# Experts' stage of a hybrid attention and mixture-of-experts block: the order of three engines written out, and a ring of 128x1024 split buffers

## The chip, the cores and the metric

The kernel runs on one core of a Trainium2 chip. The metric is the device time of one execution in microseconds, from launch to end. Three runs of the kernel before took 1589.34, 1589.37 and 1590.09 us, so the median is 1589.37 us.

## The reference

One layer over 1024 tokens of width 1024, all in float32: a token mixer (differential attention beside a causal pooling branch, merged by gates), a layer norm, a mixture of experts, a second layer norm. Only the mixture matters here:

```
g_p, g_idx = top_k(softmax(x @ w_router_group + b), 1)         # one of 4 groups
e_p, e     = top_k(softmax(expert logits of that group), 2)    # two of its 8 experts
weights    = g_p * e_p / sum(e_p)
for each expert e, for its rows xs:
    gate, up = split(xs @ w_gate_up[e], 2)                     # 1024 -> 2 x 512
    y = (silu(gate) * up) @ w_down[e]                          # 512 -> 1024
out[token] += weight * y
x = layer_norm(ALPHA * x + out)
```

## The kernel before

**Split products.** TensorE multiplies in the format fp32r, which keeps fewer bits than float32. So every operand A is split into A = hi + lo: ScalarE casts A to fp32r (hi, L150) and VectorE subtracts (lo = A - hi, L151). The helper `split` at L149 does both, and `mm3` (L164 to L167) issues three matmuls, hi*hi, hi*lo and lo*hi, into one PSUM tile.

**The experts' stage** takes the stretch from about 940 us to 1536 us. Each of the 32 experts has room for 96 rows (CAP). Its weights come from HBM in six pieces of 1 MB, 128 x 2048 float32: pieces 0 and 1 hold the gate half of `w_gate_up`, 2 and 3 the up half, 4 and 5 the two column halves of `w_down`. A piece holds four chunks of 128 x 512, one per block of 128 contraction rows. `stream` (L1044) lists the 192 pieces in the order of use, in which an expert's two down pieces stand behind the gate and up pieces of the next expert. `ahead(n)` (L1049) issues their loads on SyncE's queue in that order, each into one of NS + NM = 15 + 3 slots; a load waits until the piece 18 places earlier has been split.

For an expert, GpSimd gathers 96 rows of the normalised tokens (`gather`, L1081, tile `xg`, four buffers). TensorE turns them by eight 96x128 transposes into PSUM (tile `X`, L1039), and `split` makes `xT`. Then come `gu_half` for the gate (24 matmuls) and for the up half (24 matmuls), each into a PSUM tile `gu`; `hidden` (L1094: Silu on ScalarE, a multiplication on VectorE, tile `h`); four transposes of `h` and their split into `hT`; and `down` (24 matmuls into two PSUM tiles `dn`, each weighted into `y` by ScalarE at L1104, then a scattering DMA with addition into Y, L1105). So an expert has 72 matmuls and 12 transposes on TensorE.

**The weights' split** is done chunk by chunk: `weights_(e, c, g)` (L1061) makes one 128x512 chunk into one of five buffers `wh`, just ahead of the matmuls that use it (`product`, L1070); the first five chunks are made before the first expert (PRE = 5).

**The order of the work** in this stage is not written out. The framework's planner puts each engine's instructions in an order of its own, by program order as priority and by estimated times. In the profiled execution that order is, on TensorE: 48 gate and up matmuls, 4 down matmuls, the four transposes of this expert's `h`, the eight transposes of an `xg`, the other 20 down matmuls. `count` (L1112) works out, with three small matmuls and some VectorE operations, how many experts have more than 96 rows; `overflow` (L1136) is a loop over those. No instruction of the loop's body shows up in the trace: it runs zero times.

Of the kernel before, what the change touches and what calls it, by code (L numbers as in the profile page):

```python
# [11 lines left out]
F32 = mybir.dt.float32  # L12
# [32 lines left out]
NM = 3  # L45
M_AT = (13, 16, 17)
PRE = 5
MOE_ENG = ()
# [5 lines left out]
COUNT_AT = 1  # L54
# [55 lines left out]
def body(tc, ctx, A, out):  # L110
# [922 lines left out]
    def transposed(src, n, name, t=None):  # L1033

        t = t or turn_to(n, name)
        for g in range(0, n, 4):
            p = pt([4, CAP], "X", 3)
            for k in range(4):
                PE.transpose(p[:, k], src[:, (g + k) * 128:(g + k) * 128 + 128], ident[:CAP, :CAP])  # L1039
            split(t[:, 0, g:g + 4], t[:, 1, g:g + 4], p)  # L1040
        return t
# [17 lines left out]
    split_ = {}  # L1059

    def weights_(e, c, g):  # L1061

        if (e, c, g) in split_:
            return split_[e, c, g]
        ahead(stream.index((e, c)) + 1)
        h = split_[e, c, g] = mt([2, 512], "wh", F32R, WH_BUFS)
        split(h[:, 0], h[:, 1], pieces[e, c][:, g])
        return h

    def product(ps, x, e, c, k0):  # L1070

        for g in range(4):
            h, k = weights_(e, c, g), k0 + g
            mm3(ps, (x[:, 0, k], x[:, 1, k]), (h[:, 0], h[:, 1]), k == 0, k == (3 if c >= 4 else 7))
# [13 lines left out]
    def gu_half(e, x, c):  # L1088
        ps = pt([512], "gu", 3, CAP)
        product(ps, x, e, c, 0)  # L1090
        product(ps, x, e, c + 1, 4)
        return ps

    def hidden(h, g, u):  # L1094
        ACT.activation(h, g, AF.Silu)
        DVE.tensor_mul(h, h, u)
        return h

    def down(e, hT):
        y = rt([D], "y", F32, Y_BUFS)  # L1100
        for n in range(2):
            d = pt([512], "dn", 2, CAP)
            product(d, hT, e, 4 + n, 0)
            ACT.activation(y[:, n * 512:n * 512 + 512], d, AF.Copy, scale=wgt[:, expert[e]:expert[e] + 1])  # L1104
# [5 lines left out]
        ysc.append(q)  # L1110

    def count():  # L1112

        pc = pt([2 + 2 * NE + 1], "X", 3)
        v, b = mt([3], "cv", F32, 1)[:NE], mt([2 * NE + 1], "cb", BF, 1)[:NE]
        nb, end = v[:, 0:1], v[:, 1:2]

        PE.matmul(pc[:NE, 0:1], cum, one[:, 0:1], start=True, stop=True)
        DVE.tensor_scalar(nb, pc[:NE, 0:1], 1.0 / CAP, -0.5 - 0.5 / CAP, op0=OP.mult, op1=OP.add)
        DVE.tensor_scalar(nb, nb, MAGIC, MAGIC, op0=OP.add, op1=OP.subtract)  # L1120
        DVE.tensor_scalar(nb, nb, 0.0, None, op0=OP.max)
        DVE.tensor_copy(b[:, 2 * NE:], nb)
        PE.matmul(pc[:NE, 1:2], tri[:NE, :NE], b[:, 2 * NE:], start=True, stop=True)
        DVE.tensor_add(end, pc[:NE, 1:2], nb)
# [3 lines left out]
        po = pc[:1, 2:]  # L1128
        PE.matmul(po, one[:NE, 0:1], b, start=True, stop=True)
        ov, ovi = mt([NE], "ov", F32, 1)[:1], mt([2 * NE + 1], "ovi", I32, 1)[:1]  # L1130
# [3 lines left out]
        return ovi  # L1134

    def overflow(x, ovi):  # L1136

        n_more = nc.values_load(ovi[0:1, 2 * NE:], min_val=0, max_val=MAXB)
        with tc.For_i(0, n_more, 1) as i:
# [10 lines left out]
            def flat(src, n, name):  # L1150
                t = extra([n, CAP], name)
# [7 lines left out]
            def whole(ps, x, c, k0, last):  # L1159
                w = extra([4, 512], "we")  # L1160
# [9 lines left out]
            h = extra([512], "h")[:CAP]  # L1170
# [18 lines left out]
    with ExitStack() as order_:  # L1189
        if MOE_ENG:  # L1190
            order_.enter_context(tc.manual_schedule(engines=set(getattr(mybir.EngineType, n) for n in MOE_ENG)))
        x, h = turn_to(8, "xT"), rt([512], "h", F32, 1)
        ahead(NS + NM)
        for g in range(PRE):
            weights_(0, g // 4, g % 4)
        transposed(gx.pop(0), 8, "xT", x)
        for e in range(NE):
            if e == COUNT_AT:
                ov = count()
            if e + NXG < NE:  # L1200
                gx[e + NXG] = gather(e + NXG)
            g = gu_half(e, x, 0)
            hT = transposed(h, 4, "hT") if e else None
            u = gu_half(e, x, 2)
            hidden(h, g, u)
            if e + 1 < NE:
                x = transposed(gx.pop(e + 1), 8, "xT")
# [173 lines left out]
```

## Time and profile before

The profiled execution took 1583.73 us. Its span, from the first to the last instruction, is 1581.9 us, which leaves 1.8 us around it. It lies 5.6 us below the median of the three runs.

| what | whole span | experts' stage, 1100 to 1400 us |
|---|---|---|
| TensorE busy | 95% | 100% |
| VectorE busy | 77% | 92% |
| ScalarE busy | 63% | 89% |
| GpSimd busy | 21% | 44% |
| granted TensorE clock | 0.978 | 1.00 |
| moved by DMA | 241 GB/s | 376 to 384 GB/s, 16 engines busy all the time |

A busy share is the time in which at least one instruction of the engine was running. Matmuls overlap, so TensorE at 100% means that there is no gap between them, not that each runs at its peak: what a matmul costs is the distance between the starts of two that follow each other.

### The profile page before, as it was taken

The page shows a single profiled execution, that of the slowest core. Times are in us where ns is not written, and L with a number is a line of the kernel's source. Part 1 is how long each engine was busy: PE and PEld are TensorE (multiplying, and loading weights), DVE is VectorE, ACT ScalarE, POOL GpSimd, SP SyncE. Part 2 cuts the span into 40 slices and gives each one's busy share as a digit, 9 for nine tenths or more (in the row PEclk, how much of TensorE's full clock was granted, in tenths as well). Part 3 has the DMA queues.
Part 4 walks back from the last instruction along what each step waited for, and adds up shares of the span by engine and source line. Part 5 has one row for each costly group of instructions (what it writes and reads, how often), then busy time and mean ns, then how long its engine had stood idle before and what let it go on. Part 6 is the DMA issues. An engine that isn't in the chain of part 4 may idle for free.

```text
span 1581.9 us, 23148 instructions
## 1 busy us (share of the span) xinstructions
PE 1504.2 (95%) x7627; PEld 1188.8 (75%) x7627; DVE 1219.3 (77%) x2670; ACT 989.0 (63%) x1955; POOL 336.4 (21%) x232
## 2 busy tenths in 40 slices
PE   8999999999999999999999969999999999999970
PEld 6988888898898898888887856666666666666640
DVE  5774125988988986675567779899999899999867
ACT  4423124676676676674331128888888888888874
POOL 0001000210211210100004440344444444440010
PEclk9999999999999999999999969999999999999995
DMA  7156224855755864427475588999999999999725
GB/s 234 62 175 197 73 80 134 231 191 164 220 190 139 242 193 138 121 97 281 186 283 196 178 290 302 371 381 384 382 385 373 375 380 382 384 380 374 252 31 213
DMA packets 117034, 381.29 MB, mean 241 GB/s; under 512 B 12759, under 2 KB 43863, under 8 KB 91520
## 3 DMA queue, kind: packets, MB, share of 16 engines
q1 hardware_dynamic: 76176, 304.83, 51.5%
q0 software_dynamic: 40160, 74.14, 18.2%
q8 instruction: 61, 1.00, 0.3%
q10 hardware_dynamic: 576, 0.83, 0.2%
q14 instruction: 61, 0.50, 0.1%
HBM read 314.01 MB, written 71.35 MB: 244 GB/s over the span
## 4 chain that ended last, share of the span: by engine, by line
PE 84%; issue 7%; DVE 5%; DMA 2%; ACT 1%; POOL 1%; DVEq 0%; POOLq 0%; SPq 0%; ACTq 0%
PE gu L167 6%; PE gu L166 6%; PE gu L165 6%; PE ps L577 4%; PE pg L165 4%; PE pg L166 4%; PE pg L167 4%; PE po L628 3%; PE dn L166 3%; PE dn L167 3%; PE dn L165 3%; PE X L1039 2%; PE pv L165 2%; PE tp L613 2%; PE pv L167 2%
## 5 line engine op out<-in xcount | busy, mean ns | idle before, releaser
L151 DVE TENSOR_TENSOR wh<-we,wh 128x512 fp32r<-128x512 f32 x768 | 473.0, 683 | 13.6 <-ACT wh L150 10.4
L150 ACT CAST wh<-we 128x512 fp32r<-128x512 f32 x768 | 433.9, 621 | 24.8 <-PE gu L167 6.5
L1083 POOL DMA_INDIRECT xg<-X,idx x32 | 159.9, 4998 | 277.1 <-PE X L1039 266.9
L167 PE MATMUL gu<-wh,xT 128*96 128x512 f32 x512 | 202.8, 396 | 0.0
L165 PE MATMUL gu<-wh,xT 128*96 128x512 f32 x512 | 202.2, 395 | 0.5 <-ACT xT L150 0.5
L166 PE MATMUL gu<-wh,xT 128*96 128x512 f32 x512 | 202.1, 395 | 0.0
L151 DVE TENSOR_TENSOR w<-wraw,w 128x512 fp32r<-128x512 f32 x111 | 75.8, 687 | 92.6 <-ACT w L150 92.2
L150 ACT CAST w<-wraw 128x512 fp32r<-128x512 f32 x111 | 68.5, 621 | 117.7 <-PE pg L167 38.5
L580 ACT ACTIVATE P<-ps,stat 128x256 f32<-128x256 f32 (+7 forms) x128 | 94.8, 741 | 54.7 <-DVE stat L579 53.8
L166 PEld LDWEIGHTS gu<-wh,xT 128*96 128x96 f32 x512 | 83.1, 162 | 36.4
L165 PEld LDWEIGHTS gu<-wh,xT 128*96 128x96 f32 x512 | 83.0, 162 | 36.1 <-ACT xT L150 0.5
L167 PEld LDWEIGHTS gu<-wh,xT 128*96 128x96 f32 x512 | 83.0, 162 | 36.0 <-DVE xT L151 0.5
L166 PE MATMUL dn<-wh,hT 128*96 128x512 f32 x256 | 103.3, 404 | 1.6 <-DVE wh L151 1.5
L165 PE MATMUL dn<-wh,hT 128*96 128x512 f32 x256 | 100.8, 394 | 1.7 <-ACT wh L150 1.7
L167 PE MATMUL dn<-wh,hT 128*96 128x512 f32 x256 | 100.8, 394 | 0.0
L165 PE MATMUL pg<-xT,w 128*128 128x512 f32 x256 | 100.5, 392 | 0.0
L166 PE MATMUL pg<-xT,w 128*128 128x512 f32 x256 | 99.9, 390 | 0.0
L167 PE MATMUL pg<-xT,w 128*128 128x512 f32 x256 | 99.8, 390 | 0.0
L577 PE MATMUL ps<-K,Q 128*128 128x512 f32 (+2 forms) x384 | 98.8, 364 | 0.8 <-DVE z L464 0.8
L579 DVE TENSOR_REDUCE stat<-ps 128x1 f32<-128x256 f32 (+7 forms) x128 | 95.6, 748 | 1.1
L165 PE MATMUL pv<-w,xT 128*128 128x256 f32 x256 | 72.8, 284 | 0.0
L577 PEld LDWEIGHTS ps<-K,Q 128*128 128x128 f32 x384 | 64.7, 189 | 10.7 <-DVE z L464 1.3
(279 smaller groups left out, 3397.3 us busy)
## 6 DMA issues: line engine op xcount, KB each, us to landing
we<-in_we_dram SPq DMA_DIRECT2D x192, 1024.0 KB, 13.6
wraw<-in_w_dram SPq DMA_DIRECT2D x61, 512.0 KB, 3.8
Q<-RQ POOLq DMA_DIRECT2D x64, 256.0 KB, 5.1
RQ<-rh SPq DMA_DIRECT2D x32, 256.0 KB, 3.4
K<-RK POOLq DMA_DIRECT2D x16, 512.0 KB, 4.2
V<-RV POOLq DMA_DIRECT2D x16, 512.0 KB, 5.7
OT<-ohl SPq DMA_DIRECT2D x48, 128.0 KB, 2.3
oT<-OT POOLq DMA_DIRECT2D x6, 1024.0 KB, 10.5
```

The costliest lines, as they stand in the source:

```text
L150: ACT.copy(hi, src)
L151: DVE.tensor_sub(lo, src, r(hi))
L165: PE.matmul(ps, a[0], b[0], start=start, stop=False)
L166: PE.matmul(ps, a[0], b[1], start=False, stop=False)
L167: PE.matmul(ps, a[1], b[0], start=False, stop=stop)
L577: PE.matmul(ps[:, c:c + n], q[:, o, m, qc], Kt[h, m][:, c:c + n], start=o == 0, stop=o == 1)
L579: DVE.tensor_reduce(st_[:, m:m + 1], ps[:, :W], AX.X, OP.max, negate=True)
L580: ACT.activation(Pt[h, i][m][:, :W], ps[:, :W], AF.Exp, bias=st_[:, m:m + 1], accum_out=st_[:, 2 + m:3 + m])
L613: PE.transpose(ps[:, k], p[:, (4 * g + k) * 128:(4 * g + k) * 128 + 128], ident)
L628: PE.matmul(o[:, 0, c], Vt[h][:, a, kt], aT[kt // 4][:, kt % 4, b, c], start=j == 0, stop=j == len(parts) - 1)
L1039: PE.transpose(p[:, k], src[:, (g + k) * 128:(g + k) * 128 + 128], ident[:CAP, :CAP])
L1083: q = POOL.indirect_dma_start(out=x, out_offset=None, in_=X1, in_offset=IO(ap=idx[:, 2 * (e < NXG), expert[e]:expert[e] + 1], axis=0), bou ...
```

## The change

The experts' loop is put under a manual schedule for TensorE, ScalarE and VectorE: in it these three engines run exactly in program order. The program is rearranged to go with it. The weights are split by halves of a piece (two chunks, 128x1024) into a ring of five buffers; a count `used` goes up by one after each half's six matmuls, the next half is split there, and other operations are put into a table `todo` to be written one to three halves later. Two of the 18 load slots go (NM 3 to 1). The transposes of `h` stand behind the next expert's gate half, those of `xg` behind the up half. `count` becomes a generator whose steps are written over ten halves of expert 1, with its PSUM tile taken from tag `gu`. The overflow loop's tiles come from the slots.

```
-NM = 3
-M_AT = (13, 16, 17)
-PRE = 5
-MOE_ENG = ()
+NM = 1
+M_AT = (13,)
 WH_BUFS = 5
...
-    def transposed(src, n, name, t=None):
+    def transposes(src, n):
+        ps = []
         for g in range(0, n, 4):
-            p = pt([4, CAP], "X", 3)
+            ps.append(pt([4, CAP], "X", 3))
             for k in range(4):
-                PE.transpose(p[:, k], src[...], ident[:CAP, :CAP])
-            split(t[:, 0, g:g + 4], t[:, 1, g:g + 4], p)
-        return t
+                PE.transpose(ps[-1][:, k], src[...], ident[:CAP, :CAP])
+        return ps
+
+    def taken(t, g, p):
+        split(t[:, 0, 4 * g:4 * g + 4], t[:, 1, 4 * g:4 * g + 4], p)
...
+    parts = [(e, c, g) for e, c in stream for g in range(2)]
+    ring = deque()
+    todo = {}
+
+    def split_next():
+        if state["split"] < len(parts):
+            e, c, g = parts[state["split"]]
+            state["split"] += 1
+            ahead(stream.index((e, c)) + 1)
+            h = mt([2, 2, 512], "wh", F32R, WH_BUFS)
+            split(h[:, 0], h[:, 1], pieces[e, c][:, 2 * g:2 * g + 2])
+            ring.append(h)
+
+    def put(n, f, *a):
+        todo.setdefault(state["used"] + n, []).append(partial(f, *a))
+
+    def product(ps, x, c, k0):
+        for g in range(2):
+            h = ring.popleft()
+            for i in range(2):
+                k = k0 + 2 * g + i
+                mm3(ps, (x[:, 0, k], x[:, 1, k]), (h[:, 0, i], h[:, 1, i]), k == 0, k == (3 if c >= 4 else 7))
+            state["used"] += 1
+            split_next()
+            for f in todo.pop(state["used"], ()):
+                f()
...
+    with tc.manual_schedule(engines={mybir.EngineType.PE, mybir.EngineType.Activation, mybir.EngineType.DVE}):
         x, h = turn_to(8, "xT"), rt([512], "h", F32, 1)
         ahead(NS + NM)
+        for _ in range(WH_BUFS):
+            split_next()
+        for g, p in enumerate(transposes(gx.pop(0), 8)):
+            taken(x, g, p)
         for e in range(NE):
+            if e == 1:
+                counting, found = count(), []
+                for n in (1, 2, 5, 6, 9, 10):
+                    put(n, lambda: found.append(next(counting)))
             if e + NXG < NE:
                 gx[e + NXG] = gather(e + NXG)
+            g = gu_half(x, 0)
+            if e:
+                hT = turn_to(4, "hT")
+                put(1, taken, hT, 0, transposes(h, 4)[0])
+            put(2, ACT.activation, h, g, AF.Silu)
+            u = gu_half(x, 2)
             if e + 1 < NE:
+                x = turn_to(8, "xT")
+                for i, p in enumerate(transposes(gx.pop(e + 1), 8)):
+                    if e:
+                        put(1 + i, taken, x, i, p)
+                    else:
+                        taken(x, i, p)
+            put(3 if 0 < e < NE - 1 else 1, DVE.tensor_mul, h, h, u)
             if e:
                 down(e - 1, hT)
+        hT = turn_to(4, "hT")
+        taken(hT, 0, transposes(h, 4)[0])
+        down(NE - 1, hT)
+        for n in sorted(todo):
+            for f in todo.pop(n):
+                f()
+    ov = found[-1]
     ln2 = slot([2, D], F32, "ln2")
...
-    down(NE - 1, transposed(h, 4, "hT"))
     overflow(xgs[0], ov)
```

`down` now puts each weighting (`weighted`, with the scatter behind the second) one half later by `put(1, ...)`.

## Rows read from the trace of the kernel before

**Rows 1.** Stretches, all engines: start:end, length, busy time (count) by engine, clock, DMA.

```profile
1010.00:1500.00 490.00, 490.00 (x2248) 338.19 (x2249) 450.40 (x752) 437.36 (x806) 188.92 (x50) 1.00 1.00 372
```

**Rows 2.** Timeline, all engines: start, duration, engine, line, operation, count, [idle before <- releaser].

```profile
1210.55 0.39 PE L165 MATMUL dn<-wh,hT 128*96 128x512 f32 x1
...
1210.80 0.36 PEld L1039 LDWEIGHTS X<-cst,h 96*128 96x128 f32 x4 [0.32 <-DVE h L1096]
1210.81 0.55 PE L1039 MATMUL X<-cst,h 96*128 96x96 f32 x4
...
1211.32 1.03 PE L1039 MATMUL X<-cst,xg 96*128 96x96 f32 x8
1211.60 6.70 DVE L151 TENSOR_TENSOR wh<-we,wh 128x512 fp32r<-128x512 f32 x11
...
1212.62 6.53 POOL L1083 DMA_INDIRECT xg<-X,idx  x1 [10.05 <-PE X L1039]
1212.64 0.40 PE L167 MATMUL dn<-wh,hT 128*96 128x512 f32 x1
...
1228.86 0.39 PE L165 MATMUL dn<-wh,hT 128*96 128x512 f32 x1
```

**Rows 3.** Chain of waits, experts' stage: start, duration, engine, tile, line, count.

```profile
1009.54 1.41 PE X L1039 x12
...
1412.32 1.41 PE X L1039 x12
```

**Rows 4.** Timeline of TensorE, early in the stage.

```profile
987.32 0.39 PE L165 MATMUL gu<-wh,xT 128*96 128x512 f32 x1
987.55 0.49 PE L1039 MATMUL X<-cst,xg 96*128 96x96 f32 x4
987.83 0.45 PE L166 MATMUL gu<-wh,xT 128*96 128x512 f32 x1
988.12 0.39 PE L167 MATMUL gu<-wh,xT 128*96 128x512 f32 x1
```

**Rows 5.** Timeline of TensorE, second block from the end.

```profile
1505.27 0.47 PE L166 MATMUL dn<-wh,hT 128*96 128x512 f32 x1 [0.98 <-DVE wh L151]
```

**Rows 6.** Groups by line and form, 0 to 120 us: line, engine, operation, count | busy, mean ns.

```profile
L151 DVE TENSOR_TENSOR xT<-xr,xT 128x1024 fp32r<-128x1024 f32 x8 | 9.8, 1225 | 6.2 <-ACT xT L150 6.2
L150 ACT CAST xT<-xr 128x1024 fp32r<-128x1024 f32 x8 | 8.4, 1051 | 12.0 <-DMA xr<-in_xT_dram 12.0
```

**Rows 7.** Groups by line and form, 1010 to 1500 us.

```profile
L151 DVE TENSOR_TENSOR wh<-we,wh 128x512 fp32r<-128x512 f32 x646 | 396.7, 683 | 4.3 <-ACT wh L150 2.8
L150 ACT CAST wh<-we 128x512 fp32r<-128x512 f32 x646 | 364.1, 621 | 9.9
```

**Rows 8.** Timeline of ScalarE, start of the stage.

```profile
936.78 1.66 ACT L150 CAST wh<-we 128x512 fp32r<-128x512 f32 x3 [3.86 <-DMA Y<-yy]
941.75 0.48 ACT L150 CAST xT<-X 128x384 fp32r<-128x384 f32 x1 [3.31 <-PE X L1039]
```

**Rows 9.** Timeline of TensorE, start of the stage.

```profile
945.19 0.90 PE L1039 MATMUL X<-cst,xg 96*128 96x96 f32 x4 [2.84 <-DMA xg<-X,idx]
945.80 0.72 PE L165 MATMUL gu<-wh,xT 128*96 128x512 f32 x1
...
959.67 0.47 PE L165 MATMUL gu<-wh,xT 128*96 128x512 f32 x1 [0.46 <-ACT xT L150]
```

**Rows 10.** Timeline, all engines, end of the stage.

```profile
1529.19 0.47 PE L165 MATMUL dn<-wh,hT 128*96 128x512 f32 x1 [1.66 <-ACT wh L150]
...
1529.92 0.47 PE L166 MATMUL dn<-wh,hT 128*96 128x512 f32 x1 [0.25 <-DVE wh L151]
...
1535.71 0.39 PE L167 MATMUL dn<-wh,hT 128*96 128x512 f32 x1
```

**Rows 11.** Loads of the weights, from 1000 us on: count, issue ns, first and last issue.

```profile
L1055 SPq DMA_DIRECT2D we<-in_we_dram x157: 327/328/328, 1001.8 to 1480.1; - x157
```

**Rows 12.** Time from issue to landing of those loads, us.

```profile
DMA to landing us min/median/max: 8.8/14.2/19.2
```

More of the change, by code (lines that the diff above doesn't have):

```diff
@@ L53 @@
 NXG = 4
-COUNT_AT = 1
 ROPE_POOL = (1,)
@@ L1057, in ahead @@
             pieces[e, c] = w
[L1059 to L1074, printed above, removed]
+    parts = [(e, c, g) for e, c in stream for g in range(2)]
[21 more added lines that the diff above has]
+                f()
     ahead(13)
@@ L1086, in gather, with gu_half, scatter @@
         return x
-    def gu_half(e, x, c):
+    def gu_half(x, c):
         ps = pt([512], "gu", 3, CAP)
-        product(ps, x, e, c, 0)
-        product(ps, x, e, c + 1, 4)
-        return ps
[L1094 to L1104, printed above, removed]
+        product(ps, x, c, 0)
+        product(ps, x, c + 1, 4)
+        return ps
+    def scatter(e, y):
         q = POOL.indirect_dma_start(out=Y, out_offset=IO(ap=idx[:, 1, expert[e]:expert[e] + 1], axis=0), in_=y, in_offset=None,
@@ L1110, in down, with weighted @@
         ysc.append(q)
+    def weighted(e, y, n, d):
+        ACT.activation(y[:, n * 512:n * 512 + 512], d, AF.Copy, scale=wgt[:, expert[e]:expert[e] + 1])
+        if n:
+            scatter(e, y)
+    def down(e, hT):
+        y = rt([D], "y", F32, Y_BUFS)
+        for n in range(2):
+            d = pt([512], "dn", 2, CAP)
+            product(d, hT, 4 + n, 0)
+            put(1, weighted, e, y, n, d)
     def count():
-        pc = pt([2 + 2 * NE + 1], "X", 3)
+        pc = pt([512], "gu", 3)[:, :2 + 2 * NE + 1]
+        ov, ovi = mt([NE], "ov", F32, 1)[:1], mt([2 * NE + 1], "ovi", I32, 1)[:1]
         v, b = mt([3], "cv", F32, 1)[:NE], mt([2 * NE + 1], "cb", BF, 1)[:NE]
@@ L1122, in count @@
         DVE.tensor_copy(b[:, 2 * NE:], nb)
+        yield
         PE.matmul(pc[:NE, 1:2], tri[:NE, :NE], b[:, 2 * NE:], start=True, stop=True)
+        yield
         DVE.tensor_add(end, pc[:NE, 1:2], nb)
@@ L1128, in count @@
         po = pc[:1, 2:]
+        yield
         PE.matmul(po, one[:NE, 0:1], b, start=True, stop=True)
-        ov, ovi = mt([NE], "ov", F32, 1)[:1], mt([2 * NE + 1], "ovi", I32, 1)[:1]
+        yield
         DVE.tensor_copy(ovi, po)
@@ L1133, in count @@
         DVE.tensor_scalar(ovi[:, NE:2 * NE], ov, 1.0, float(CAP), op0=OP.add, op1=OP.mult)
-        return ovi
+        yield ovi
     def overflow(x, ovi):
@@ L1150, in flat @@
             def flat(src, n, name):
-                t = extra([n, CAP], name)
+                t = slot([n, CAP], F32, name)
                 for g in range(0, n, 4):
@@ L1188, in body @@
             store_rows(j)
-    with ExitStack() as order_:
-        if MOE_ENG:
-            order_.enter_context(tc.manual_schedule(engines=set(getattr(mybir.EngineType, n) for n in MOE_ENG)))
+    state.update(split=0, used=0)
+    with tc.manual_schedule(engines={mybir.EngineType.PE, mybir.EngineType.Activation, mybir.EngineType.DVE}):
         x, h = turn_to(8, "xT"), rt([512], "h", F32, 1)
         ahead(NS + NM)
-        for g in range(PRE):
-            weights_(0, g // 4, g % 4)
-        transposed(gx.pop(0), 8, "xT", x)
+        for _ in range(WH_BUFS):
+            split_next()
+        for g, p in enumerate(transposes(gx.pop(0), 8)):
+            taken(x, g, p)
         for e in range(NE):
-            if e == COUNT_AT:
-                ov = count()
+            if e == 1:
+                counting, found = count(), []
+                for n in (1, 2, 5, 6, 9, 10):
+                    put(n, lambda: found.append(next(counting)))
             if e + NXG < NE:
                 gx[e + NXG] = gather(e + NXG)
[L1202 to L1205, printed above, removed]
-            if e + 1 < NE:
-                x = transposed(gx.pop(e + 1), 8, "xT")
+            g = gu_half(x, 0)
[4 more added lines that the diff above has]
+            u = gu_half(x, 2)
+            if e + 1 < NE:
+                x = turn_to(8, "xT")
[5 more added lines that the diff above has]
+            put(3 if 0 < e < NE - 1 else 1, DVE.tensor_mul, h, h, u)
             if e:
                 down(e - 1, hT)
+        hT = turn_to(4, "hT")
[5 more added lines that the diff above has]
+    ov = found[-1]
     ln2 = slot([2, D], F32, "ln2")
```

8 lines of the change are left out of this document (4 added, 4 removed).

## The prediction

> **What bounds the kernel now.** I read the stretches first, over the steady part of the experts' stage [rows 1]. Of 490 us TensorE is busy 490.00, VectorE 450.40 (92%), ScalarE 437.36 (89%); the granted clock is 1.00, so TensorE stays at its level of 2.4 GHz, and the DMA engines are busy all the time at 372 GB/s. TensorE has no gap there, so the stage can only end sooner if TensorE does the same work in less time, or starts or ends better. The chain of waits gives the period: the block of twelve transposes returns 22 times between 1009.54 and 1412.32 us [rows 3], every 402.78 / 22 = 18.31 us, once per expert.
>
> Then the timeline of one period says what TensorE does in it [rows 2]. After the block, from the matmul at 1212.64 to the one at 1228.86, lie 70 distances: 0.2317 us per matmul. An expert's 72 matmuls are worth 72 x 0.2317 = 16.68 us; 1.63 us are left for twelve transposes. The block shows the same number: from the last matmul before it (1210.55) to the second behind it (1212.64) are 2.09 us, less two matmuls 1.63. Inside, four transposes take 1210.81 to 1211.32 and eight about 1.0 more: 0.127 us each. The row of the weight load tells why I doubt that this is their price: the block's first load had to wait for VectorE's `h`, which is made just before, out of the last up matmul. Where nothing is waited for, early in the stage [rows 4], four transposes start at 987.55 and the next matmul at 987.83; from 987.32 to 988.12 are 0.80 us, less two matmuls 0.34, which is 0.084 per transpose with the change-over paid. So in the steady block the loads don't run ahead of the matmuls any more, once the first was late, and each short transpose shows its load.
>
> **The change, part by part.** All durations are of the profiled execution (1583.73 us); I subtract the sum from it and, as the same difference, from the median, 1589.37.
>
> *A, the transposes.* The new order puts the four of `h` behind the next gate half; `h` was finished at least four halves (5.6 us) before. The eight of `xg` stand behind the up half and need rows gathered four experts ahead. Nothing is late for either, so I take the price of rows 4: 12 x 0.084 = 1.01 us instead of 1.63, 0.62 saved. The block of twelve occurs 27 times (22 periods from the first on in rows 3, then to the last but two experts); the block of expert 30 follows, where TensorE waits 0.98 us for a split [rows 5], which the deeper ring removes: 27 x 0.62 + 1.0 = 17.7 us. Bounds: -0.8 (each transpose stays at 0.127, and two change-overs of 0.07 instead of one cost 0.03 more per expert than now) and 22.5 (0.28 / 4 = 0.07 each, no change-over: 0.84 per expert).
>
> *B, the start.* The first matmul, 945.80, stands behind four transposes of expert 1 that wait 2.84 us for a second gather [rows 9]. In the new order they come 48 matmuls later. ScalarE has the first `xT` at 941.75 + 0.48 = 942.2 [rows 8]. But five wide splits stand ahead of it: ScalarE's casts start at 936.78 when space comes free (5 x 1.051 = 5.3, so 942.0), VectorE's remainders end at 936.78 + 1.05 + 5 x 1.225 = 944.0 [rows 6], its `xT` at 944.5. The third matmul waits for that, which is as if the stream had begun at 944.0: 1.8 earlier, less 0.34 for the four transposes now paid elsewhere, 1.5 us. Bounds 0 (one more buffer comes free late) and 3.4 (stream from 942.4).
>
> *C, expert 0 to 1.* `down` doesn't lie between yet, so `xT` of expert 1 is wanted at once. Before, the wait was 0.46 us [rows 9], about 0.7 with the remainder. Now a wide cast stands ahead of ScalarE's `xT` and a wide remainder ahead of VectorE's: 1.05 + 0.48 less 0.67 for the eight transposes, then 0.8 for the remainder, about 1.7: 1.0 us lost; bounds 0 and 2.
>
> *D, the end.* The last `down` waits 1.66 us, then twice 0.25 [rows 10], because its splits are made only now: 2.2 in all. With the ring full, only four transposes, a cast and a remainder of about 0.5 each (as in rows 8) are in the way: 0.9. With 0.3 for the unwaited transposes 1.6 us gained; bounds 0.5 and 2.5.
>
> *E, half as many splits, each twice as wide.* Per expert VectorE has 12 x 1.225 = 14.7 us and (450.40 - 396.7) / 26.8 = 2.0 of other work [rows 1, 7], 16.7; ScalarE 12 x 1.051 + (437.36 - 364.1) / 26.8 = 15.3. Both lie under the new period, 16.68 + 1.01 = 17.69. I cost this at nothing, because TensorE hides it. What is added is a wait for a whole half: the split of the half five places on is issued when a half ends, and must be ready four halves (4 x 1.39 = 5.56 us) later. It takes 1.05 + 1.23 and some 0.3 of hand-over; operations put beside it (Silu, `hT`, `xT`, the product) delay it by at most three of about 0.6. Some 1 us is left at the worst place. Behind a late split stand, on ScalarE and VectorE, all later splits, and TensorE waits for them in order.
>
> *F, the loads.* 16 slots instead of 18 cut the reserve by two pieces. 157 loads are issued 478.3 us apart from first to last, and land 8.8 to 19.2 us later [rows 11, 12], so they land every 3.00 to 3.13 us, while the new period asks for one every 17.69 / 6 = 2.95. The reserve shrinks, but does it last? The seventeenth load can go when the first piece is split, about 940, and land at 945; the last then at 945 + 175 x 3.08 = 1484. TensorE ends at 1535.71 + 0.23 [rows 10] - 20 = 1516; the last piece's second split must start its work seven halves and 2.4 us sooner, at 1504. 20 us are over: cost nothing. They would be used up at 3.19 us per load.
>
> *G, the rest.* `count` still has three matmuls and the same small operations; the `ln2` loads move behind the last `down` in program order, but have some 20 us until the second norm; the overflow loop doesn't run. Nothing, within 1 us.
>
> Sum: 17.7 + 1.5 - 1.0 + 1.6 = 19.8 us. 1583.73 - 19.8 = 1563.9 profiled; on the median's level 1589.37 - 19.8 = **1569.5 us**. With the terms' own bounds this case lies between 1564 and 1575.
>
> **The rivals.** *R1, the transposes stay at 0.127.* A gives -0.8 + 1.0, the rest 2.1: 1587 us. For it: every one of the 22 periods has that price. Against: in rows 4 the same operation on the same operands costs less, between the same matmuls, and the only difference I see is the wait for `h`. The Trainium skill speaks for it (TensorE: Matmul & The Clock Gate, The mechanism): a weight load runs beside a matmul in flight only where the two use different row groups, and here both use the same rows. By that rule the loads could never be hidden, and the result would be this rival's; rows 4 contradict it.
>
> *R2, the loads bind.* For it: DMA is busy all the time in rows 1, and the loads' landing is the slowest series of the stage but for TensorE. At 3.25 us per load the last lands at 1514, 10 us after its need: 1579 us. Against: it takes a rate 6% under the one shown.
>
> *R3, slower: VectorE becomes the bound.* With 12 x + 2.0 us per expert it passes the new period at x = 1.31 and the old one, 18.31, at x = 1.36 us per wide remainder; at 1.45 the period is 19.4, and 31 experts cost 34 us: 1589 - 2 + 34 = 1621. For it: 92% busy now, in fixed order, and GpSimd's gathers of 6.53 us run beside it. Against: during that gather [rows 2] eleven remainders took 6.70 us, 0.61 each, no more than elsewhere, and the wide form measured 1.225 with the space between two included.
>
> *R4, nothing moves.* The hand-overs of 384 halves, 0.05 us each, eat the 19 us: 1589. Against: a semaphore that is already up costs no gap in rows 2 (70 matmuls at one distance, with a wait every three).
>
> **How the numbers follow.** Chances: forecast 0.70, R1 0.09, R2 0.08, R3 0.07, R4 0.06. No change means within 0.2%, 3.2 us, about what a measurement of this kernel can tell. R1 at 1587 lies at that edge, so half of it counts as faster: faster 0.70 + 0.08 + 0.05 = 0.83, same 0.04 + 0.06 = 0.10, slower 0.07. The range goes from 1562 (A near its upper bound, B at 3.4) to 1585, which takes in R2 and leaves out R1, R3 and R4 and a little below.
>
> **What would show it.** Period 17.7 us instead of 18.3, two runs of transposes per expert with 0.08 us or less each, and no wait of their loads on `h` (A); first gate matmul near 942.5 with a wait of its third (B); a wait near 956 before expert 1 (C); one wait near 1507 (D); VectorE under 95% busy, casts of 1.05 and remainders of 1.2 (E); no wait for a load, landing times growing to over 20 us (F). I am wrong if TensorE waits at halves for `wh`, if transposes stay at 0.127, or if ScalarE waits for the loads.

## The result, and the profile after

The changed kernel took 1574.22 us (median of four runs, 1571.85 to 1575.4) where the kernel before took 1589.73 us beside it: ratio 0.990, 95% interval 0.9883 to 0.9917, so 15.5 us less (13.2 to 18.6 by that interval). The forecast was 1569.5 us, 19.8 less. The profiled execution of the changed kernel took 1573.52 us, span 1571.7, which is 10.2 us less than the profiled execution before.

In the changed kernel L147 and L148 are the split, L162 to L164 `mm3`, L1036 the transposes, L1087 Silu and the product `h`, L1096 the gather, L1108 the scatter. The steady stretch, in the columns of [rows 1]:

```profile
1010.00:1500.00 490.00, 490.00 (x2333) 348.56 (x2332) 444.80 (x443) 414.79 (x499) 117.20 (x52) 1.00 1.02 378
```

TensorE still has no gap, VectorE has 91% and ScalarE 85%, the clock is 1.00. So the steady gain must lie in what TensorE does without a gap. The timeline of TensorE shows where the transposes went (compare [rows 2]):

```profile
1206.91 0.49 PE L1036 MATMUL X<-cst,h 96*128 96x96 f32 x4
1207.19 0.45 PE L162 MATMUL gu<-wh,xT 128*96 128x512 f32 x1
...
1212.81 0.82 PE L1036 MATMUL X<-cst,xg 96*128 96x96 f32 x8
1213.42 0.45 PE L162 MATMUL dn<-wh,hT 128*96 128x512 f32 x1
```

The four of `h` stand between two gate and up matmuls, the eight of `xg` between the last of these and the first of `down`. Four take 0.28 us until the next matmul, eight 0.61: 0.07 to 0.08 each; the block of twelve before took 1.52 by the same measure (1210.81 to the next matmul, 1212.33). The scatters of GpSimd give the period (answering to [rows 3]; start, duration, line, [idle before <- releaser]):

```profile
1028.12 3.35 POOL L1108 DMA_INDIRECT Y<-y,idx  x1 [7.64 <-ACT y L1116]
...
1487.62 3.32 POOL L1108 DMA_INDIRECT Y<-y,idx  x1 [14.34 <-ACT y L1116]
```

26 periods in 459.50 us are 17.67 us each; 18.31 before, 17.69 forecast.

The start is what went the other way. First VectorE, GpSimd and TensorE in the changed kernel, then the same place in the kernel before:

```profile
937.68 0.38 DVE L1021 SCALAR_TENSOR_TENSOR idx<-first,no 96x32 int32<-96x32 f32 x3
937.98 5.75 DVE L148 TENSOR_TENSOR wh<-we,wh 128x1024 fp32r<-128x1024 f32 x5
938.79 5.87 POOL L1096 DMA_INDIRECT xg<-X,idx  x1 [8.53 <-ACT wh L147]
944.96 0.99 POOL L1096 DMA_INDIRECT xg<-X,idx  x1 [0.30 <-issue]
951.09 1.54 PE L1036 MATMUL X<-cst,xg 96*128 96x96 f32 x8 [14.04 <-DMA xg<-X,idx]
952.55 0.74 PE L162 MATMUL gu<-wh,xT 128*96 128x512 f32 x1
```

```profile
935.45 0.38 DVE L1024 SCALAR_TENSOR_TENSOR idx<-first,no 96x32 int32<-96x32 f32 x3
935.76 0.68 DVE L151 TENSOR_TENSOR wh<-we,wh 128x512 fp32r<-128x512 f32 x1
936.65 1.05 POOL L1083 DMA_INDIRECT xg<-X,idx  x1 [9.01 <-DVE wh L151]
937.43 1.90 DVE L151 TENSOR_TENSOR wh<-we,wh 128x512 fp32r<-128x512 f32 x3 [0.99 <-ACT wh L150]
```

In both, GpSimd starts the first gather 0.7 to 0.8 us after VectorE has made `idx`. Before, it began in a gap of 0.99 us on VectorE and took 1.05 us. After, VectorE runs five remainders without a gap until 943.73, and the gather's instruction takes 5.87 us, until 944.66. The rows land late, TensorE stands for 14.04 us, and the first gate matmul comes at 952.55 instead of 945.80 [rows 9].

The instruction is not all of it. From its end to the first transposes it is 6.43 us, where it was 3.11 before (937.70 to 940.81). Two loads of weights, into slots that the first remainders have set free, are under way in that time (issues first and last, then a stretch of all engines):

```profile
L1055 SPq DMA_DIRECT2D we<-in_we_dram x2: 328/328/328, 940.4 to 942.6; - x2
944.00:946.00 2.00, 0.00 (x0) 0.00 (x0) 0.00 (x0) 0.00 (x0) 1.65 (x2) 0.50 1.01 414
```

The DMA engines are busy all the time, and the loads land 4.8 and 7.0 us after their issue, the second at 949.6; the first expert's rows land at 951.1, 12.3 us after the gather began. In the kernel before the first such load was issued at 939.36, 1.66 us after the gather's instruction had ended.

The passage from expert 0 to 1, ScalarE and then TensorE:

```profile
963.98 1.28 ACT L1087 ACT_TABLE_LOAD   x1
965.27 0.59 ACT L1087 ACTIVATE h<-gu 96x512 f32<-96x512 f32 x1
965.77 1.98 ACT L147 CAST wh<-we 128x1024 fp32r<-128x1024 f32 x2
967.65 0.85 ACT L147 CAST xT<-X 128x384 fp32r<-128x384 f32 x2
```

```profile
968.17 0.48 PE L162 MATMUL gu<-wh,xT 128*96 128x512 f32 x1 [1.86 <-ACT xT L147]
968.49 0.39 PE L163 MATMUL gu<-wh,xT 128*96 128x512 f32 x1
969.72 0.52 PE L164 MATMUL gu<-wh,xT 128*96 128x512 f32 x1 [0.84 <-DVE xT L148]
970.04 0.63 PE L162 MATMUL gu<-wh,xT 128*96 128x512 f32 x1
```

`xT` stands behind two wide casts, and these behind the first Silu, which had to load its table first. TensorE waits 1.86 + 0.84 us, and then its matmuls take 0.63 instead of 0.39: the clock has fallen. Two stretches show TensorE's work and the granted clock there (the first begins with the slow first gate matmuls of expert 0):

```profile
950.00:970.00 20.00, 16.22 (x67) 11.26 (x68) 11.63 (x12) 11.78 (x14) 4.91 (x5) 0.84 0.73 227
970.00:990.00 20.00, 20.00 (x89) 13.36 (x88) 15.44 (x26) 13.90 (x17) 2.31 (x1) 0.91 0.79 280
```

The end, against [rows 10], then the splits in the steady stretch, against [rows 6, 7], and the loads, against [rows 11, 12]:

```profile
1519.85 0.47 PE L162 MATMUL dn<-wh,hT 128*96 128x512 f32 x1 [0.57 <-ACT hT L147]
...
1525.48 0.39 PE L164 MATMUL dn<-wh,hT 128*96 128x512 f32 x1
```

```profile
L148 DVE TENSOR_TENSOR wh<-we,wh 128x1024 fp32r<-128x1024 f32 x334 | 400.6, 1220 | 45.2 <-ACT wh L147 41.6 <-DMA we<-in_we_dram 0.2
L147 ACT CAST wh<-we 128x1024 fp32r<-128x1024 f32 x333 | 349.5, 1050 | 75.2 <-PE gu L164 47.3 <-PE dn L164 27.9
```

```profile
L1055 SPq DMA_DIRECT2D we<-in_we_dram x161: 327/328/328, 1001.9 to 1486.2; - x161
...
DMA to landing us min/median/max: 9.0/22.7/28.0
```

One wait of 0.57 us is left in front of the last `down`, the wide splits cost what the rows of the first 120 us said, and no split waits for a load but for 0.2 us once.

**Where the 10.2 us of the two profiles are.** `idx` 2.2 us later (935.45 to 937.68); from there to the first gate matmul 4.5 us more (10.35 to 14.87); from it to the last down matmul 17.0 us less (589.91 to 572.92); behind it the same (46.2 each). The first term is not the change: the code ahead of the stage is the same in all kernels here, and their profiled executions reach `idx` between 935.09 (e1_start) and 939.74 us (b1_xt2). In the changed kernel's execution VectorE waited 1.1 us for a load of `x` near 853 us, TensorE then stood 1.37 us instead of 0.40, and the clock fell; in the kernel before it did not (both rows are 860 to 870 us, before and after):

```profile
860.00:870.00 10.00, 10.00 (x56) 8.12 (x54) 10.00 (x70) 1.50 (x6) 4.06 (x5) 1.00 0.80 261
```

```profile
860.00:870.00 10.00, 10.00 (x47) 7.83 (x47) 8.56 (x63) 1.18 (x5) 3.23 (x5) 0.83 0.65 234
```

So the two profiles flatter the kernel before, by these 2.2 us at least, and the change itself is worth 12.5 us between them (17.0 - 4.5). The medians say 15.5; where the 3 us between lie is not shown, as no profile shows one of the longer executions of the kernel before. The mean granted clocks on record go with them: the profiled execution before had 0.978; of fifteen later executions of that kernel, those with 0.977 or 0.978 took 1584.8 to 1587.6 us and those with 0.974 or 0.975 took 1589.9 to 1590.6; the four of the changed kernel had 0.974 or 0.975.

### The profile page after: what moved, and what is told of

Read it like the earlier page. It is cut to its first block, busy times and chain, and to the rows that moved or that the text cites. A ratio compares the mean times of both kernels' runs of the same rounds, so it can differ in the third digit from the quotient of the medians.

```text
span 1571.7 us, 22002 instructions
## 1 busy us (share of the span) xinstructions
PE 1488.5 (95%) x7627; PEld 1188.9 (76%) x7627; DVE 1196.7 (76%) x2286; ACT 946.8 (60%) x1571; POOL 272.8 (17%) x232
## 4 chain that ended last, share of the span: by engine, by line
PE 52%; issue 31%; POOL 9%; DVE 5%; DMA 2%; ACT 1%; POOLq 0%; DVEq 0%; SPq 0%; ACTq 0%
POOL Y L1108 6%; PE ps L574 4%; PE pg L162 4%; PE pg L163 4%; PE pg L164 4%; PE po L625 3%; POOL xg L1096 2%; PE pv L162 2%; PE tp L610 2%; PE pv L164 2%; PE pv L163 2%; PE pB L162 2%; PE pB L163 2%; PE pB L164 2%; PE pa L162 2%
## 5 line engine op out<-in xcount | busy, mean ns | idle before, releaser
L148 DVE TENSOR_TENSOR wh<-we,wh 128x1024 fp32r<-128x1024 f32 x384 | 460.3, 1219 | 57.7 <-ACT wh L147 53.7
L147 ACT CAST wh<-we 128x1024 fp32r<-128x1024 f32 x384 | 402.5, 1049 | 92.9 <-PE gu L164 61.4
L162 PE MATMUL gu<-wh,xT 128*96 128x512 f32 x512 | 204.9, 400 | 1.9 <-ACT xT L147 1.9
L164 PE MATMUL gu<-wh,xT 128*96 128x512 f32 x512 | 203.3, 397 | 0.8 <-DVE xT L148 0.8
L1108 POOL DMA_INDIRECT Y<-y,idx x32 | 104.7, 3272 | 271.9 <-ACT y L1116 267.1
L148 DVE TENSOR_TENSOR w<-wraw,w 128x512 fp32r<-128x512 f32 x111 | 75.8, 686 | 92.4 <-ACT w L147 91.9
L147 ACT CAST w<-wraw 128x512 fp32r<-128x512 f32 x111 | 68.5, 621 | 117.9 <-PE pg L164 38.5
L164 PEld LDWEIGHTS gu<-wh,xT 128*96 128x96 f32 x512 | 83.2, 162 | 37.5 <-DVE xT L148 1.5
L162 PEld LDWEIGHTS gu<-wh,xT 128*96 128x96 f32 x512 | 83.2, 163 | 35.5 <-ACT xT L147 2.3
L162 PE MATMUL dn<-wh,hT 128*96 128x512 f32 x256 | 102.5, 400 | 0.6 <-ACT hT L147 0.6
L164 PE MATMUL dn<-wh,hT 128*96 128x512 f32 x256 | 100.9, 394 | 0.0
L162 PE MATMUL pg<-xT,w 128*128 128x512 f32 x256 | 100.5, 392 | 0.0
L164 PE MATMUL pg<-xT,w 128*128 128x512 f32 x256 | 99.8, 390 | 0.0
L162 PE MATMUL pv<-w,xT 128*128 128x256 f32 x256 | 72.8, 284 | 0.0
```

Source lines behind the costliest of these rows:

```text
L147: ACT.copy(hi, src)
L148: DVE.tensor_sub(lo, src, r(hi))
L162: PE.matmul(ps, a[0], b[0], start=start, stop=False)
L164: PE.matmul(ps, a[1], b[0], start=False, stop=stop)
```

## The experiments

All times are medians, all ratios are to the kernel before on the same chip, with their 95% interval. The medians of the kernel before lay at 1587.8 to 1589.7 us beside the several groups of kernels, so a gain over the changed kernel is given by the medians and, in brackets, by the ratios (0.990 less the kernel's, times 1589).

### e1_start: is it VectorE that holds the first gather?

```
...
-        for _ in range(WH_BUFS):
-            split_next()
+        later = []
+        for i in range(WH_BUFS):
+            split_next(later if i else None)
         for g, p in enumerate(transposes(gx.pop(0), 8)):
             taken(x, g, p)
+        for f in later:
+            f()
```

With a list, `split_next` issues the cast and puts the remainder into the list.

> The changed kernel with one edit: of the five first wide splits, all casts and the first remainder stay ahead of the first expert's xT, the other four remainders come behind it on VectorE. Theory V: in the changed kernel the first gather's instruction on GpSimd took 5.87 us (938.79 to 944.66) because VectorE ran five remainders back to back (937.98 to 943.73), and GpSimd gets to write the descriptors only when VectorE leaves a gap. Then the instruction takes 1.0 to 1.4 us here (1.05 in the kernel before), the transposes of the first xg start about 4.2 us after it begins instead of 12.3, the first gate matmul comes 7 to 8 us earlier, and the time is about 1574.2 - 7.5 = 1567 us. Rival S: the gather is slow because of ScalarE's five casts, or because the transfer itself is slow behind the weights' loads; then the instruction stays near 5.9 us or the landing late, the first matmul does not move, and the time stays at 1574 us.

1566.43 us, ratio 0.9867 (0.9851 to 0.9882): 7.8 us (5.2) less than the changed kernel. VectorE, GpSimd and TensorE:

```profile
935.39 1.21 DVE L148 TENSOR_TENSOR wh<-we,wh 128x1024 fp32r<-128x1024 f32 x1
...
936.20 1.33 POOL L1100 DMA_INDIRECT xg<-X,idx  x1 [8.92 <-ACT wh L1073]
...
940.94 1.54 PE L1036 MATMUL X<-cst,xg 96*128 96x96 f32 x8 [6.49 <-DMA xg<-X,idx]
942.41 0.74 PE L162 MATMUL gu<-wh,xT 128*96 128x512 f32 x1
```

The gather's instruction takes 1.33 us and ends at 937.53, 0.93 us after the one remainder ahead of it (936.60); in the changed kernel it ended 0.93 us after the fifth. ScalarE's five casts are where they were, so they are not the cause. From `idx` to the first gate matmul it is 7.3 us instead of 14.9, 7.5 less. Theory V holds for the instruction, and that is 4.5 of the 7.5 us.

The other 3.0 us lie between the instruction's end and the first transposes, 3.41 us instead of 6.43. Here the edit does a second thing: four remainders later also means load slots set free later, and the next load of weights is issued only at 944.79, when the rows have landed:

```profile
944.79 13.31 SPq L1055 DMA_DIRECT2D we<-in_we_dram  x6
```

So the slow transfer of rival S was there too. The profiles of all kernels agree: with no load of weights issued between `idx` and the end of the gather's instruction this time is 3.1 to 3.5 us (the kernel before, e1_start, e6_both, e9_warm), with one 5.0 to 5.5 (e5_expert1, e7_ring3, b1_xt2), with two 5.6 to 7.2 (the changed kernel, e2, e3, e4, e8). The two shares are read from the traces; no run moves one without the other.

### e5_expert1 and e6_both: the passage to expert 1, and both edits together

```
...
+        ACT.activation(mt([1], "silu", F32, 1), eps, AF.Silu)
         for g, p in enumerate(transposes(gx.pop(0), 8)):
...
+            if e == 0:
+                x1 = slot([2, 8, CAP], F32R, "xT")
+                for i, p in enumerate(transposes(gx.pop(1), 8)):
+                    put(2 + i, taken, x1, i, p)
             u = gu_half(x, 2)
-            if e + 1 < NE:
+            if e == 0:
+                x = x1
+            elif e + 1 < NE:
...
```

> The changed kernel with the xT of expert 1 made during the up half of expert 0, into a free load slot, and with Silu's table fetched by a small Silu ahead of the first expert. In the changed kernel TensorE stands 2.04 + 1.0 us there (965.25 to 969.72 us), because the table's load (1.28 us) and two wide casts lie between the first Silu and xT on ScalarE, and the clock falls to 1.2 GHz for 3.4 us just after. Theory C: both go, 3.0 us of waits and 1.5 us of slow matmuls: 1574.2 - 4.5 = about 1570 us, and no wait between expert 0 and 1. Rival: the wait is only moved, because the second xT or the first transposes of h are late next, or the lost slot binds: 1573 to 1576 us.

1566.95 us, ratio 0.9871 (0.9853 to 0.9888): 7.3 us (4.6) less. The waits between expert 0 and 1 are gone, and from the first gate matmul to the last down matmul it is 568.72 us, 4.2 less than in the changed kernel. That and the ratio bear out the expected 4.5. From `idx` to the first gate matmul it is 13.5 us instead of 14.9 here; the edit takes a load slot, and one load of weights is issued beside the first gather instead of two. The rest of what the medians show is not explained.

> The changed kernel with both edits: four of the five first remainders behind the first xT, and the xT of expert 1 and Silu's table early. If the two losses are independent, the gains add: 1574.2 - 7.8 - 4.5 = about 1562 us. If the start is limited by something that both share (the first gathers' rows, the clock that rises only some time after the matmuls begin), the sum is smaller: 1565 us or more.

1561.64 us, ratio 0.983 (0.9814 to 0.9845): 12.6 us (11.1) less than the changed kernel, and 27 less than the kernel before, the best version with e9_warm below. The sum of the two gains would be 15.1 (9.8). The profile has both: 7.4 us from `idx` to the first gate matmul, and 568.76 from it to the last down matmul. The first of the two stretches shown above, in this kernel:

```profile
950.00:970.00 20.00, 20.00 (x95) 13.82 (x94) 19.25 (x25) 15.85 (x19) 3.67 (x3) 1.00 1.00 369
```

Between 950 and 970 us TensorE has no gap and the clock is 1.00, where the changed kernel had 16.22 us of work at 0.84.

### e2_late_h and e3_twelve: was it the late load, or the long block?

e2 makes `h` right behind the up half and puts the twelve transposes behind two halves of `down`, so that their first load waits for `h` as in the kernel before:

```
...
+                DVE.tensor_mul(h, h, u)
+                turned = []
+                def middle(e=e):
+                    turned.extend(transposes(h, 4))
+                    if e + 1 < NE:
+                        turned.append(turn_to(8, "xT"))
+                        for i, p in enumerate(transposes(gx.pop(e + 1), 8)):
+                            put(1 + i, taken, turned[1], i, p)
+                down(e - 1, hT, middle)
...
```

> The changed kernel with h multiplied right behind the up half and its four transposes, with the eight of xg behind them, put behind the first two halves of the down product, so that the block of twelve has its first load wait for h again, as in the kernel before. Theory A: the wait is what makes the transposes dear. Each costs 0.127 us instead of 0.083, which is 0.53 us per expert, and TensorE also stands 0.2 to 0.4 us for h itself: period 18.4 to 18.6 us instead of 17.67, 30 experts, 22 to 28 us more, 1596 to 1602 us. Rival B: no price hangs on the wait; then only the wait itself shows, period 17.9 to 18.1 us, 1581 to 1587 us.

1626.48 us, ratio 1.0241 (1.0227 to 1.0255), period 19.4 us: longer than either expected. TensorE at the block:

```profile
1236.03 0.52 PE L1036 MATMUL X<-cst,h 96*128 96x96 f32 x4 [0.32 <-DVE h L1238]
1236.38 0.82 PE L1036 MATMUL X<-cst,xg 96*128 96x96 f32 x8
1236.99 0.45 PE L162 MATMUL dn<-wh,hT 128*96 128x512 f32 x1
```

The load waited for `h`, and still the twelve take 1236.03 to 1236.99 = 0.96 us, 0.08 each. Theory A of this test, which is the prediction's reason, falls. Most of the extra time is elsewhere, by the distances of the starts: 0.49 us of standing for `h`, and 0.85 and 0.24 us at each expert's first gate matmuls, from an `xT` that my edit makes too late.

e3 keeps the twelve together, unwaited:

```
                 put(1, taken, hT, 0, transposes(h, 4)[0])
+                if e + 1 < NE:
+                    turned = transposes(gx.pop(e + 1), 8)
...
-                for i, p in enumerate(transposes(gx.pop(e + 1), 8)):
+                for i, p in enumerate(turned if e else transposes(gx.pop(e + 1), 8)):
```

> The changed kernel with the eight transposes of the next xg put right behind the four of h, after the gate half, so that TensorE has one block of twelve per expert again, but none of its loads waits for anything. Theory A (a late first load is what made the block of the kernel before dear): the block costs twelve times 0.07 plus one change-over, about 0.95 us, period 17.6 to 17.7 us, time 1572 to 1575 us, the same as the changed kernel. Rival C (a long block is dear, because its PSUM tiles or its loads pile up): the block costs 1.63 us as before, period 18.3 us, 31 times 0.63, about 1593 us.

1573.89 us, ratio 0.99 (0.9884 to 0.9917), period 17.65 us: the same as the changed kernel. A long block isn't dear either.

### b1_xt2 and e8_held: are the tiles X held?

What is left is in the timeline of the kernel before, between the lines of [rows 2]:

```profile
1210.07 0.68 DVE L1096 TENSOR_TENSOR h<-h,gu 96x512 f32<-96x512 f32 x1 [1.33 <-PE gu L167]
...
1210.67 1.01 DVE L151 TENSOR_TENSOR xT<-X,xT 128x384 fp32r<-128x384 f32 x2
...
1211.83 0.52 PE L1039 MATMUL X<-cst,xg 96*128 96x96 f32 x4
...
1212.33 0.16 PEld L166 LDWEIGHTS dn<-wh,hT 128*96 128x96 f32 x1 [0.17 <-DVE wh L151]
```

`xT` has one buffer, so the two X tiles filled at the last block are only read now, when the up half has let go of it. VectorE's two remainders end at about 1211.2 and 1211.7, and the eight transposes, which write those tiles, start right after: the first four at 1211.32, the second four at 1211.83. Their row is 1.03 us long where a free eight have 0.82. The matmul behind the block, at 1212.33, waits 0.17 us for a remainder of `wh` queued behind both. So each group of four takes 0.50 or 0.51 us until the next start, where the twelve of e2 take 0.35 for the first four and 0.61 for the other eight. b1 gives the kernel before a second `xT` buffer:

```
-NM = 3
-M_AT = (13, 16, 17)
+NM = 2
+M_AT = (13, 16)
...
-XT_BUFS = 1
+XT_BUFS = 2
```

> The kernel before with two buffers for xT instead of one (and 17 load slots instead of 18 to make room); the planner then spreads the transposes of xg over three places per expert. Theory X: what made the twelve transposes of the kernel before cost 1.63 us was not that their loads were late, but that the PSUM tiles X of the block were still held: xT has one buffer, so the X tiles filled one expert earlier are only split once the up half is done, and the second and third group of four wait for VectorE's two remainders of xT (done at 1211.22 and 1211.68 us, the loads at 1211.29 and 1211.80), the down matmul behind the block for the remainder of wh queued behind them. With a second buffer the X tiles come free early: twelve transposes at 0.082 and some change-overs, about 1.1 to 1.3 us, period 17.8 to 18.0 us instead of 18.31, 27 blocks, 9 to 14 us less than before, 1575 to 1580 us. Rival O: only the written order removes such waits, the planner's order keeps VectorE late at the block: period 18.2 to 18.4 us, 1585 to 1592 us.

1603.51 us, ratio 1.0095 (1.008 to 1.011), period 18.84 us: both expectations missed. The transposes of `h` and the first of `xg`, whose load waits for `h`, and who waited for whom from 1100 to 1300 us (us in total, times, longest):

```profile
1204.05 0.55 PE L1039 MATMUL X<-cst,h 96*128 96x96 f32 x4
...
1204.43 0.41 PE L1039 MATMUL X<-cst,xg 96*128 96x96 f32 x3
```

```profile
PEld gu L166 <- DVE wh L151: 14.7, 30, 0.9
```

With the tiles free, the transposes are cheap behind a late load here too (0.38 us from the four to the next, 0.22 for three of `xg`). But the planner's new order makes the gate matmuls wait for their splits, 30 times in 11 experts, and that costs more. So b1 supports the reading at the block, and is no way to get the gain.

e8 adds the held tiles to e2: the block turns the `xg` of two experts on, and both `xT` splits come behind `h`:

```
...
+                DVE.tensor_mul(h, h, u)
+                if e + 1 < NE:
+                    x = turn_to(8, "xT")
+                    for i, p in enumerate(held):
                         taken(x, i, p)
...
+                turned = []
+                def middle(e=e):
+                    turned.extend(transposes(h, 4))
+                    if e + 2 < NE:
+                        turned.extend(transposes(gx.pop(e + 2), 8))
+                down(e - 1, hT, middle)
+                held = turned[1:]
...
```

> The changed kernel brought closer to what the kernel before does at its block of twelve: h is multiplied right behind the up half, the eight transposes stand for the xg of two experts on, so that their PSUM tiles X stay filled for a whole expert, and both xT splits, which free them, come behind h on VectorE, just before the block. Theory X: the held tiles are what made the block dear. The first four transposes go at 0.082 us each although their load waited for h, the fifth waits for VectorE's first remainder of xT and the ninth for the second: block of 1.2 to 1.6 us where e2_late_h had 0.96, and with some 0.5 us of standing for h a period of 18.4 to 18.8 us, 1596 to 1610 us. Rival Y: tiles that are held cost nothing, the block stays at 0.96 us as in e2_late_h; only the standing for h remains: period 18.1 to 18.3 us, 1587 to 1594 us.

1598.22 us, ratio 1.0051 (1.0037 to 1.0064), period 18.44 us. VectorE and TensorE at the block:

```profile
1208.68 1.01 DVE L148 TENSOR_TENSOR xT<-X,xT 128x384 fp32r<-128x384 f32 x2
...
1208.91 0.52 PE L1036 MATMUL X<-cst,h 96*128 96x96 f32 x4 [0.32 <-DVE h L1239]
1209.33 1.03 PE L1036 MATMUL X<-cst,xg 96*128 96x96 f32 x8
1210.15 0.45 PE L162 MATMUL dn<-wh,hT 128*96 128x512 f32 x1
```

The same twelve now take 1208.91 to 1210.15 = 1.24 us, 0.28 more than in e2, half of the 0.56 by which the kernel before lies over e2 (1.52 to 0.96). With 0.49 of standing for `h` that is the period: 17.67 + 0.49 + 0.28 = 18.44. Theory X holds for this part. Of the other half, 0.09 us lies in the first four (0.51 us until the next start before, 0.42 here) and 0.19 in the eight (1.01 before, 0.82 here), which in the kernel before end in the printed wait of 0.17 us for the remainder of `wh`.

### e4_narrow and e7_ring3: the width and the depth of the ring

```
-WH_BUFS = 5
+WH_BUFS = 10
...
-    parts = [(e, c, g) for e, c in stream for g in range(2)]
+    parts = [(e, c, g) for e, c in stream for g in range(4)]
...
```

Here `split_next` makes one 128x512 chunk and is called twice per half.

> The changed kernel with the splits made by chunks of 128x512 again, two after each half, into a ring of ten such buffers (the same bytes); the order is otherwise unchanged. Theory E: the width does nothing for the steady stage, because VectorE (24 x 0.61 + 2.0 = 16.7 us per expert) and ScalarE (24 x 0.55 + 2.2 = 15.4 us) stay under TensorE's 17.67: period 17.67 us, time 1573 to 1576 us. Rival W: the halved count of instructions is what gives the slack, and with 128x512 some splits come late in the fixed order: waits of TensorE at halves, period 17.9 to 18.3 us, 1581 to 1593 us.

1571.94 us, ratio 0.9893 (0.9878 to 0.9908), period 17.67 us: the width does nothing for the steady stage. (The first gather takes 6.21 us here, behind ten narrow remainders.)

e7 changes only `WH_BUFS`, from 5 to 3.

> The changed kernel with a ring of three 128x1024 buffers instead of five. The prediction left about 1 us of slack at the worst place with five. Theory E: with three, a split must be ready two halves (2.78 us) after its place comes free, takes 1.05 + 1.2 + 0.3 us, and wherever Silu, hT, xT or the product lies beside it (about 5 of the 12 halves of an expert, 0.3 to 0.7 us each) TensorE stands: period 18.5 to 20.5 us, 1600 to 1660 us. Rival: the slack is larger than thought, the fixed order alone keeps the ring full: period under 17.9 us, 1574 to 1580 us.

1585.78 us, ratio 0.9984 (0.9974 to 0.9994), period 18.07 us, between the two expectations. Waits from 1010 to 1500 us:

```profile
PEld gu L163 <- DVE wh L148: 22.5, 54, 0.6
```

Two of an expert's twelve halves come late, not five. With three buffers nearly the whole gain is gone, so a depth of more than three is needed; the width is not.

### e9_warm: keep TensorE busy while it waits

This adds to e6_both the block of twelve of e3_twelve and twelve idle matmuls ahead of the first transposes:

```
...
+        idle = pt([512], "dn", 2, CAP)
+        for _ in range(12):
+            PE.matmul(idle, ring[0][:, 0, 0, :CAP], ring[0][:, 0, 0], start=True, stop=True)
         for g, p in enumerate(transposes(gx.pop(0), 8)):
...
```

> e6_both with two more edits: twelve matmuls of no use on the first split buffer, while TensorE waits for the first xg (about 936 to 942 us), and the block of twelve transposes of e3_twelve. In the changed kernel the granted clock is at 1.2 GHz until 3.7 us after the first gate matmul, and eight matmuls take 0.43 instead of 0.23 us, the eight transposes 0.5 us more. If busy TensorE is what brings the clock back, the first gate matmuls run at 2.4 GHz: 1.6 + 0.5 us, and 0.02 us per expert from the one block: 1561.6 - 2.7 = about 1559 us. If the clock needs something else, or the idle matmuls hold up the first transposes, nothing is gained: 1561 to 1564 us.

1560.9 us, ratio 0.9824 (0.9811 to 0.9837), no different from e6_both. Two stretches, around the first transposes and behind them:

```profile
941.50:943.00 1.50, 1.26 (x10) 0.90 (x10) 0.45 (x1) 0.86 (x2) 1.20 (x2) 1.00 0.97 292
943.30:946.50 3.20, 3.20 (x8) 2.11 (x9) 3.20 (x4) 1.05 (x1) 2.59 (x3) 0.50 0.68 160
```

The transposes of the first expert do run at 2.4 GHz, but TensorE had stood 1.29 us for the gather between the idle matmuls and them, and the clock then falls to 1.2 GHz under the first gate matmuls. The gain is given back.

## Why the prediction was right, and where it was wrong

**A, the transposes (17.7 forecast): the size right, the reason wrong.** The period is 17.67 us, 0.64 less than before; times 27, and 1.0 for expert 30, that makes 18.3. But "the loads don't run ahead of the matmuls any more, once the first was late" is false: e2_late_h has a late first load and pays 0.08 per transpose. What was dear were the tiles X, read too late by VectorE because of the one `xT` buffer (0.28 us per block in e8_held), and by the rows of the block the remainder of `wh` behind them (0.17 us of wait); this last part was read from the rows and not tested by itself. That the size came out is no luck, as it was taken from measured rows, but any reason for the difference between rows 2 and rows 4 would have given the same number. I had compared the block with [rows 4], where both the wait for `h` and the held tiles are absent, and named only the difference that had a wait printed beside it. The eight transposes at 1.03 us in [rows 2] had no printed wait and were late all the same: compare lengths, not only waits.

**B, the start (+1.5): the wrong sign.** The step that failed is the first `xT` at 942.2: I took the gather's landing from [rows 8] as if nothing ahead of it moved, and counted the five wide remainders only as work ahead of `xT` on VectorE. They hold GpSimd, and the slots that they set free start two loads of weights ahead of the gathered rows. It cost 4.5 us where 1.5 were to be gained, and e1_start takes 7.5 off that stretch: 4.5 from the instruction, 3.0 from what follows its end. [Rows 2] had shown it: the gather of 6.53 us ends 0.85 us after the run of eleven remainders. In rival R3 I read this row only for what the gather does to VectorE (nothing), not for what VectorE does to the gather. The Trainium skill has the rule (SBUF — State Buffer, section SBUF: two separate sides): a DMA issued by GpSimd needs GpSimd to write its descriptors, and VectorE locks it out of the port they share while it runs an operation in a 2-port mode, or one with two SBUF inputs against a GpSimd operation that reads SBUF. The traces agree that the gather waits for the remainders, which have two inputs: 5.87 us against 1.05 and 1.33. That it is this port they do not show.

**C, expert 0 to 1 (-1.0): the size.** Waits of 2.7 us by the rows instead of the 1.7 I had worked out, as two casts and Silu's table (1.28 us) stand ahead of `xT`, not one cast; and a fall of the clock that the forecast did not have, with nine matmuls at 0.43 us, 1.7 more. Against 0.7 before, 3.7 lost; e5_expert1 gives 4.2 back.

**D, the end (+1.6): right.** TensorE's waits there go from 2.2 us [rows 10] to 0.57 and 0.13 at the third matmul, and the four transposes are unwaited.

**E and F (nothing): right.** The casts take 1.05 us and the remainders 1.22, VectorE 91%, and e4_narrow is the same time with the old width. TensorE waits for no load; they take up to 28.0 us to land and come at 378 GB/s.

The rivals: R1 (0.127 stays) is refuted by the new rows. The rule of the Trainium skill that spoke for it (TensorE: Matmul & The Clock Gate, The mechanism) doesn't hold here as I quoted it: a load of 96x128 lasts 0.14 us, and transposes on the same rows start every 0.08 us, even behind a late load. The same section also lets a load go ahead into a background weight buffer; that fits these rows, and I had left it out. R2 and R3 did not come. R4 did not either: 12 hand-overs per expert cost nothing in a period that is 72 x 0.2317 + 0.99.

The sum of the stage: 18.3 (A) + 1.8 (D: 2.2 - 0.7 + 0.3) - 3.7 (C) = 16.4 of the 17.0 measured from the first gate matmul to the last down matmul (0.6 are left over), less 4.5 at the start. The forecast came close to the medians because A, by far the largest term, was right in size; that the medians lie only 4.3 us from it is in part luck, as between the profiles the change is worth 12.5 us and not 19.8. The 1564 to 1575 given with the sum does not follow from the terms' bounds: the lower ones with A at 17.7 give 1573, the upper ones all together 1561.

## What to carry to other kernels

Look at what runs on VectorE while GpSimd issues a DMA that something waits for: leave a gap there. Look also at which loads start at that place, as they can move ahead of the rows that are waited for. When a group of short instructions is dear, compare its length with the same group elsewhere and ask which buffers it writes, and who reads them last. Written orders move the first and last passage of a stage too; beside a steady gain of 18 us, those two places were worth 11 to 13 more.

## What the runs showed of the hardware

GpSimd's gather instruction took 1.0 us alone and as long as VectorE had two-input remainders without a gap: 1.33 us behind one of 128x1024 (e1_start), 3.60 behind three (e7_ring3), 5.87 behind five, 6.21 behind ten of 128x512 (e4_narrow) and 6.53 beside eleven [rows 2], ending 0.85 to 0.93 us after the last of them; one gap of 0.99 us was enough.

The first gathered rows came later when loads of weights had been issued before the gather's instruction ended: 3.1 to 3.5 us from that end to the transposes without such a load, 5.0 to 5.5 with one, 5.6 to 7.2 with two.

The granted clock fell from 2.4 to 1.2 GHz shortly after TensorE had stood for 1 to 3 us (near 860 us, behind 969.72, and in e9_warm), and at the last two places matmuls then take 0.43 instead of 0.23 us for some microseconds. A short wait of TensorE can so cost more than its length. Not each one does: in the kernel before, TensorE stood 1.54 us ahead of 846.90 and 1.66 ahead of 1529.19 [rows 10], and the clock stayed at 2.4 GHz for the next 10 us.
